# A hybrid encoder layer on one NeuronCore: the order of the attention stage made by a list scheduler inside the kernel

## The chip, the core and the metric

The kernel runs on one core of one Trainium2 chip. The metric is the device time of one execution in microseconds, taken as the median of several runs. One execution was also recorded by the hardware profiler; its span runs from the first recorded instruction to the last and is a little shorter than the time of that execution. Engines are called PE (matmul), ACT, DVE, POOL and SP; SP only issues transfers here, and ACT and POOL issue some too.

## The reference, cut to what matters

One encoder layer in float32 over two requests, 512 and 256 tokens of width 2048, with shared weights. The 768 tokens are handled together as six blocks of 128 rows.

```python
h = rmsnorm(x); z = h @ w_in                      # columns: fourier 1024 | q 1024 | k 256 | v 256
of = einsum('bsgc,gcd->bsgd', fft2(zf).real, w_f) # 8 groups of 128 channels
s  = q @ k.T * 64**-0.5, masked to |i-j| <= 128   # 16 q heads, 4 kv heads, head_dim 64, rotary
m  = max(s, sink); p = exp(s-m) / (sum(exp(s-m)) + exp(sink-m)); oa = p @ v
x  = x + concat(rmsnorm(of), rmsnorm(oa)) @ w_out
h  = rmsnorm(x); x = x + relu(h @ w_up)**2 @ w_down   # d_ff = 8192
y  = rmsnorm(x)
```

## The kernel before, in words

Every float32 operand is split into two parts, high and low, whose sum is the value (`split`, L62: ACT writes the high part, DVE the difference). A product is then three matmuls: high by high, high by low, low by high.

The stages follow each other in time. Up to about 399 us PE makes the projections (L481). Beside them DVE, ACT and POOL do the Fourier groups (`fold`, `stage1`, `stage2`), whose results go to DRAM (`of_d`, L347), and the rotation of keys and queries. From 399 to 634 us runs the attention stage (L501 to L739). From 634 to 780 us comes the second half of the output projection (L780), then the up projection (L888) and the down projection (L1163), both in a form with seven products instead of eight.

In the attention stage PE has two kinds of work. The first half of the output projection, the part that takes the Fourier result, is 24 slots (four column blocks `n` by six row blocks `m`) of 24 matmuls each: eight steps `k` of three (L693). It needs nothing from attention and fills PE between the attention pieces. Attention is 24 units, a unit being one block of 128 queries with one kv head, four q heads. In a unit PE makes the scores (`qk`, L522), DVE adds the mask and takes the row maximum (L535), ACT takes the exponentials (L552), DVE sums and inverts (L562), POOL normalises (L565), PE transposes each key block (`trans`, L577), ACT and DVE split it (L580, L581), and PE multiplies it with the values (`pv`, L596). Blocks at the edges of a request see two key blocks of 128, the others three: 16 units have two, 8 have three, 56 key blocks in all. The low half of the result is added to the high half by ACT and DVE (L603, L606) and stored (`oa_d`). When the four units of a row block are stored, `load_oa` (L626) reads it back, splits it and sums its squares for the norm.

The order before: PE's order is the order of the program text everywhere, SP's also in this stage, and the other engines are ordered by the framework. The text order comes from a heap of events with fixed times counted in steps `k` of the projection (`at`, `later`, `run_events`, L651 to L680): unit `u` starts at step 7.52 `u`, its transposes 8.38 steps later, and so on. After every step of three matmuls, the events due are issued.

PSUM has eight banks. Before, the scores of a head take one of four banks `s`; the transposes `t` and the result `o` share two banks (tag `t`); the projection has two (`mm`).

The Fourier result is read back as float32 (`load_of`, L682, tile `ofr`) and split in the attention stage. The queries of three of the four kv heads lie in DRAM already split; `load_q` reads them into `rx`, and ACT copies them to `qs` (L440).

At the start of the second half each pair of row blocks (a half-step, `mp`) gets its partial result `y1_d` and the residual `x` by two SP loads, which POOL adds (L798); the sum is needed by DVE at the end of the half-step (L816). At the border from up to down the first unit of down lies in buffers of the up stage (`factor_tile`, L1115); the second is loaded, summed and split in buffers that are free only later (`loads(1)`, `sums(1)`, `lows(1)`).

Of the kernel before, what the change touches and what calls it, by code (L numbers as in the profile page):

```python
# [29 lines left out]
FG = 8  # L30
# [10 lines left out]
def hybrid_encoder(ctx: ExitStack, tc: tile.TileContext, a: dict):  # L41
# [3 lines left out]
    def f32(ap):  # L45
        return ap.bitcast(F32)

# [67 lines left out]
    of_d = dpool.tile([FG * P, T], F32, tag="of", name="ofd")  # L115
    oa_d = [dpool.tile([NH * HD, P], F32, tag=f"oa{i}", name=f"oad{i}") for i in range(NM)]
# [31 lines left out]


    kctx = ExitStack()  # L150
    with ExitStack() as ph:
# [175 lines left out]
        def stage2(g):  # L327
# [18 lines left out]
            nc.scalar.activation(of[:], of[:], AF.Copy, scale=gcat[:, g : g + 1])  # L346
            nc.scalar.dma_start(of_d[g * P : (g + 1) * P, :], of[:])  # L347
# [54 lines left out]
        def queries(g, i, s):  # L402
# [4 lines left out]
            lo = kt["kp"].tile([P, HALF], F32, tag="rl", name="rl")  # L407
            split(hi[:], lo[:], x, HD ** -0.5)
            nc.scalar.dma_start(qr_d[g][0][rs, t0], f32(hi[:]))
            nc.scalar.dma_start(qr_d[g][1][rs, t0], lo[:])  # L410
# [4 lines left out]
        def load_q(u):  # L415
# [3 lines left out]
            x = kt["kp"].tile([P, 4, P], F32, tag="rx", name="rx", bufs=2)  # L419
            state[u] = {"x": x}  # L420
            if g < NKV - 1:
                nc.sync.dma_start(x[0:64], rows(qr_d[g][0]))
                nc.sync.dma_start(x[64:128], rows(qr_d[g][1]))
                return
            y = kt["kp"].tile([P, 4, P], F32, tag="ry", name="ry", bufs=2)
            nc.sync.dma_start(x[0:64], rows(zq_d[g]))
            nc.sync.dma_start(y[0:32], rows(zq_d[g])[32:64])
            nc.sync.dma_start(y[32:64], rows(zq_d[g])[0:32])
            state[u]["y"] = y

        def rotate_q(u):
            b, g = units[u]
            if g == NKV - 1:
                rotate(state[u]["x"][:HD], state[u].pop("y")[:HD], slice(b * P, (b + 1) * P))

        def split_q(u):
            x = state[u].pop("x")
            qs = state[u]["qs"] = kt["kp"].tile([P, 4, P], F32R, tag="qs", name="qs", bufs=2)
            if units[u][1] < NKV - 1:
                nc.scalar.activation(qs[:], x[:], AF.Copy)  # L440
                return
            nc.scalar.activation(qs[0:64], x[0:64], AF.Copy, scale=HD ** -0.5)
            nc.vector.scalar_tensor_tensor(
                out=qs[64:128], in0=x[0:64], scalar=HD ** -0.5, in1=f32(qs[0:64]), op0=ALU.mult, op1=ALU.subtract
            )
# [20 lines left out]
        for u in range(2):  # L466
            after(32.5 + u, lambda u=u: (load_q(u), split_q(u)))
# [41 lines left out]
    def key_blocks(b):  # L509
        lo, hi = (0, 3) if b < 4 else (4, 5)  # L510
        return max(lo, b - 1), min(hi, b + 1)

    def qk(u, heads):
        b, g = units[u]
        k0, k1 = key_blocks(b)
        nk = (k1 - k0 + 1) * P
        st = state[u]
        for h in heads:
            s = pp3.tile([P, 512], F32, tag="s", name="s", bufs=4)
            st[f"s{h}"] = s  # L520
            for n, kd in enumerate((kdl, kdh)):
                nc.tensor.matmul(s[:, :nk], st["qs"][:, h, :], kd[:, g, k0 * P : k0 * P + nk], start=(n == 0), stop=(n == 1))  # L522

    def row_max(u, heads):
        b, g = units[u]
        k0, k1 = key_blocks(b)
        nk = (k1 - k0 + 1) * P
        off = (k0 - b + 1) * P
        st = state[u]
        if "mx" not in st:  # L530
            st["mx"] = ap_.tile([P, 4], F32, tag="mx", name="mx")
        mx = st["mx"]
        for h in heads:
            s = st[f"s{h}"]
            nc.vector.tensor_tensor_reduce(  # L535
                out=s[:, :nk], in0=s[:, :nk], in1=mask[:, off : off + nk], scale=1.0,
                scalar=sink[:, 4 * g + h : 4 * g + h + 1], op0=ALU.add, op1=ALU.max, accum_out=mx[:, h : h + 1],
            )

    def exps(u):  # L540
        b, g = units[u]
# [814 lines left out]
```

## Time and profile before

| | us |
|---|---|
| median of 3 runs (lowest, highest) | 2648.18 (2647.71, 2649.71) |
| the profiled execution, its own time | 2648.75 |
| its span | 2647.0 |
| PE busy in the span | 2604.1 (98%) |
| DVE, ACT, POOL busy | 1729.4, 1059.4, 260.2 |
| attention stage on PE | 399.4 to 634.0 |
| granted PE clock, mean | 0.997 |

How to read it: a matmul's recorded duration is longer than its distance to the next, since matmuls overlap, so PE is busy in the record even where it is issued late. The spacing of starts tells more than the busy share. A row of the timeline shows the start, the duration, the engine, the line and the operation; in square brackets stands the idle time before it and what ended that.

### The profile page before, as it was taken

Reading aid. Unit: us, or ns where it says so; the run is one execution under the profiler, and the core shown is the slowest. Engines: PE = TensorE matmul, PEld = TensorE weight load, DVE = VectorE, ACT = ScalarE, POOL = GpSimd, SP = SyncE. Lnnn points to the kernel's source line nnn. Section 1 sums busy time; section 2 is a strip of 40 time slices with the busy share of each in tenths; the row PEclk is TensorE's granted clock in tenths of the full one; section 3 lists DMA queues with packets and bytes.
Section 4 is the critical chain, followed back from the end, with each engine's and each line's share of the span. In section 5 each row is a group of like instructions: output and inputs, shape, how many; then the busy total and the mean of one; then the engine's idle time right before and its main releaser. Section 6 shows DMA issues by size and latency. Waiting matters only on the chain.

```text
span 2647.0 us, 35016 instructions
## 1 busy us (share of the span) xinstructions
PE 2604.1 (98%) x13652; PEld 2375.5 (90%) x13652; DVE 1729.4 (65%) x2100; ACT 1059.4 (40%) x1523; POOL 260.2 (10%) x369
## 2 busy tenths in 40 slices
PE   8999999998999999999999999999999999999998
PEld 8999997877889999999999999978888888888886
DVE  6334456766746655555787778757776775777677
ACT  5233326664423343333445444433333333333335
POOL 1011212334310010100000000020000000000000
PEclk9999999999999999999999999999999999999999
DMA  5323465444564454547666666585553672554364
GB/s 172 122 94 110 134 203 153 121 128 149 198 216 165 165 178 158 191 160 270 227 228 219 216 225 234 179 332 175 175 171 100 207 258 68 179 184 158 101 207 145
DMA packets 263398, 468.31 MB, mean 177 GB/s; under 512 B 26240, under 2 KB 157824, under 8 KB 262464
## 3 DMA queue, kind: packets, MB, share of 16 engines
q1 hardware_dynamic: 199232, 314.26, 37.2%
q10 hardware_dynamic: 51792, 101.73, 10.0%
q0 software_dynamic: 12208, 50.08, 5.6%
q8 instruction: 107, 1.75, 0.3%
q14 instruction: 59, 0.48, 0.1%
HBM read 345.67 MB, written 120.32 MB: 176 GB/s over the span
## 4 chain that ended last, share of the span: by engine, by line
PE 75%; DMA 4%; DVE 3%; issue 3%; ACT 1%; POOL 1%; SPq 1%; ACTq 0%; POOLq 0%; DVEq 0%
PE pd L1163 34%; PE pu L888 34%; PE pm L693 6%; PE o L596 1%; PE t L577 1%; PE s L522 1%; DMA ry<-zq 1%; DMA ofr<-ofd 1%; ACT p L552 1%; DMA zq<-zs 0%; DVE s L535 0%; DMA oar<-oad 0%; PE ptx L131 0%; DMA raw<-in_w_out 0%; DMA qh<-rh 0%
## 5 line engine op out<-in xcount | busy, mean ns | idle before, releaser
L888 PE MATMUL pu<-xf,wh 128*128 128x384 f32 x3328 | 848.7, 336 | 0.0
L888 PEld LDWEIGHTS pu<-xf,wh 128*128 128x128 f32 x3328 | 600.5, 188 | 1.8 <-ACT o L906 1.3
L888 PE MATMUL pu<-xf,wl 128*128 128x384 f32 x1664 | 559.1, 336 | 0.0
L1163 PE MATMUL pd<-wl,sh 128*128 128x512 f32 x1332 | 518.9, 390 | 2.4 <-DVE wl L1152 2.4
L1163 PE MATMUL pd<-wh,sl 128*128 128x512 f32 x1332 | 518.9, 390 | 1.5 <-DVE sl L1153 1.5
L1163 PE MATMUL pd<-wh,sh 128*128 128x512 f32 x1332 | 518.9, 390 | 0.0
L1142 ACT ACTIVATE wh<-rd 128x1024 fp32r<-128x1024 f32 x200 | 201.9, 1054 | 531.0 <-PE pd L1163 436.0
L1152 DVE TENSOR_TENSOR wl<-rd,wh 128x1024 fp32r<-128x1024 f32 x200 | 236.0, 1221 | 234.2 <-ACT wh L1142 233.6
L868 ACT ACTIVATE wh<-ur 128x1024 fp32r<-128x1024 f32 x160 | 169.9, 1062 | 374.2 <-PE pu L888 214.1
L888 PEld LDWEIGHTS pu<-xf,wl 128*128 128x128 f32 x1664 | 312.8, 188 | 0.0
L1163 PEld LDWEIGHTS pd<-wl,sh 128*128 128x128 f32 x1332 | 250.4, 188 | 55.0 <-DVE wl L1152 2.8
L1163 PEld LDWEIGHTS pd<-wh,sl 128*128 128x128 f32 x1332 | 250.4, 188 | 53.9 <-DVE sl L1153 1.8
L1163 PEld LDWEIGHTS pd<-wh,sh 128*128 128x128 f32 x1332 | 250.3, 188 | 51.9
L874 DVE TENSOR_TENSOR wl<-ur,wh 128x1024 fp32r<-128x1024 f32 x160 | 195.5, 1222 | 82.6 <-ACT wh L868 82.5
L909 DVE TENSOR_TENSOR o<-pu,o 128x768 f32<-128x768 f32 x160 | 153.0, 956 | 116.9 <-PE pu L888 111.1
L481 PE MATMUL pz<-hh,wh 128*128 128x384 f32 x576 | 147.1, 336 | 0.0
L481 PE MATMUL pz<-hl,wh 128*128 128x384 f32 x576 | 146.3, 334 | 0.0
L481 PE MATMUL pz<-hh,wl 128*128 128x384 f32 x576 | 146.2, 334 | 0.0
L1135 DVE TENSOR_TENSOR rd<-rd 128x1024 f32<-128x1024 f32 x112 | 131.8, 1218 | 0.0
L868 ACT ACTIVATE wh<-sx 128x1024 fp32r<-128x1024 f32 x64 | 67.9, 1062 | 127.8 <-PE pu L888 97.0
L66 DVE TENSOR_TENSOR wl<-raw,wh 128x1024 fp32r<-128x1024 f32 x56 | 68.8, 1235 | 65.8 <-ACT wh L65 63.2
L1153 DVE TENSOR_TENSOR sl<-sr,sh 128x768 fp32r<-128x768 f32 x111 | 105.6, 951 | 0.0
(208 smaller groups left out, 3558.8 us busy)
## 6 DMA issues: line engine op xcount, KB each, us to landing
rd<-in_w_down SPq DMA_DIRECT2D x176, 512.0 KB, 5.1
ur<-in_w_up SPq DMA_DIRECT2D x128, 512.0 KB, 3.9
sr<-sd SPq DMA_DIRECT2D x95, 384.0 KB, 5.3
pd<-o ACTq DMA_DIRECT2D x64, 384.0 KB, 2.3
o<-pd POOLq DMA_DIRECT2D x64, 384.0 KB, 6.1
sd<-sm ACTq DMA_DIRECT2D x60, 384.0 KB, 2.9
raw<-in_w_in SPq DMA_DIRECT2D x40, 512.0 KB, 3.6
raw<-in_w_out SPq DMA_DIRECT2D x32, 512.0 KB, 5.0
```

What stands on the lines that cost most here:

```text
L66: nc.vector.tensor_tensor(out=lo, in0=src, in1=f32(hi), op=ALU.subtract)
L481: nc.tensor.matmul(ps[c][s][:, :HALF], w[:, i, cs], h[j][:, i, s * HALF : (s + 1) * HALF], start=first and n == 0, stop=last and n == 2,)
L693: nc.tensor.matmul(ps[:], l(k), w[:, k % 2, :], start=(k == 0 and n == 0), stop=(k == 7 and n == 2))
L868: nc.scalar.activation(wh[:], raw[:], AF.Copy)
L874: nc.vector.tensor_tensor(out=wl[:], in0=raw[:], in1=f32(wh[:]), op=ALU.subtract)
L888: nc.tensor.matmul(ps[:, t, :HALF], w[:, i, t * P : (t + 1) * P], xb[:, o, i, :], start=(s == first_of[bank] and i == 0 and n == 0), stop= ...
L909: nc.vector.tensor_tensor(out=o, in0=src, in1=o, op=ALU.add)
L1135: add = lambda x, y, op: nc.vector.tensor_tensor(out=x[:], in0=x[:], in1=y[:], op=op)
L1142: nc.scalar.activation(wh[:], t[:], AF.Copy)
L1152: nc.vector.tensor_tensor(out=wl[:], in0=t[:], in1=f32(wh[:]), op=ALU.subtract)
L1153: nc.vector.tensor_tensor(out=sl[:], in0=sr[:], in1=f32(sh[:]), op=ALU.subtract)
L1163: nc.tensor.matmul(ps[m][:, ns], l[:, q, ts], w[:, ns], start=(j == 0 and q == 0 and t == 0), stop=(j == HP // 2 - 1 and q == 1 and t == 2),)
```

## The change

It has five parts.

1. The attention stage gets a list of jobs. A job has a key, an engine, a cost in us, a due time, a function, the jobs it comes after, an earliest start and a wait until its result can be used. `in_turn` makes a list schedule of them while the program is built (at each step the job that can start first, ties by due time), and the jobs are issued in that order. In this stage ACT, DVE, POOL and SP now follow the text order too, not PE and SP alone. The pieces of a unit become single jobs, four row maxima, four exponentials and so on. The negated maxima are made in two instructions of two columns, not one of four.
2. PSUM: the scores have three banks, and a unit with two key blocks puts two heads into one bank; `o` has a bank of its own, the transposes two.
3. The Fourier result is split in `stage2` and stored as two tensors, which the attention stage loads straight into place. Queries that lie split in DRAM are loaded straight into `qs` (three buffers). The attention result is stored in two unadded halves; `oa_load` loads one and adds the other on the way by an accumulating transfer of the POOL queue. The partial results `y1` are stored by SP.
4. In the second half the residual is loaded by SP, and `y1` is added on it by an accumulating transfer of the POOL queue.
5. Down's second unit is loaded into buffers of up, summed and half split before down begins; two weight pieces that are kept for later are loaded a second time.

The diff, cut ("..." marks what is left out):

```diff
-    of_d = dpool.tile([FG * P, T], F32, tag="of", name="ofd")
-    oa_d = [dpool.tile([NH * HD, P], F32, tag=f"oa{i}", name=f"oad{i}") for i in range(NM)]
+    of_d = [dpool.tile([P, NM, FG, P], F32, tag=f"of{c}", name=f"ofd{c}") for c in "hl"]
+    oa_d = [[dpool.tile([NH * HD, P], F32, tag=f"oa{c}{i}", name=f"oad{c}{i}") for c in "hl"] for i in range(NM)]
...
-            nc.scalar.activation(of[:], of[:], AF.Copy, scale=gcat[:, g : g + 1])
-            nc.scalar.dma_start(of_d[g * P : (g + 1) * P, :], of[:])
+            split(ofh[:], ofl[:], of[:], gcat[:, g : g + 1])
+            for c, x in enumerate((ofh, ofl)):
+                nc.scalar.dma_start(of_d[c][:, :, g, :], f32(x[:]).rearrange("p (m t) -> p m t", m=NM))
...
         for u in range(2):
-            after(32.5 + u, lambda u=u: (load_q(u), split_q(u)))
+            after(32.5 + u, lambda u=u: load_q(u))
+        for i in range(2):
+            after(32.5 + i, lambda i=i: (out_load(i), out_split(i)))
...
+    def maxima(u, step):
...
+            hs = slice(2 * step, 2 * step + 2)
+            nc.vector.tensor_scalar(out=st["nm"][:, hs], in0=st["mx"][:, hs], scalar1=-1.0, scalar2=None, op0=ALU.mult)
...
+    def oa_load(m, c):
+        for i in range(2):
+            src = oa_d[m][c][i * 512 : (i + 1) * 512, :].rearrange("(k p) t -> p k t", p=P)
+            if c == 0:
+                oar[m, i] = (op, ap_)[i].tile([P, 4, P], F32, tag="oar", name="oar", bufs=2)
+                nc.sync.dma_start(oar[m, i][:], src)
+            else:
+                nc.gpsimd.dma_start(oar[m, i][:], src, accum_op=ALU.add)
...
+    def load_of(m):
+        for c in range(2):
+            nc.sync.dma_start(f32(ofs[m][c][:]), of_d[c][:, m])
...
+    def in_turn(hop, slack):
...
+        while ready:
+            key = min(ready, key=lambda x: (max(ready[x], free.get(jobs[x][0], -1e9)), jobs[x][2], number[x]))
+            engine, cost, _, _, _, _, wait = jobs[key]
+            t = starts[key] = max(ready.pop(key), free.get(engine, -1e9))
+            free[engine], ends[key] = t + cost, t + cost + wait
+            order.append((t, len(order), key))
+            for x in users[key]:
+                blocked[x] -= 1
+                if not blocked[x]:
+                    late = hop + (slack if jobs[x][0] == PE and x[0] != "mm" else 0)
+                    ready[x] = max([jobs[x][5]] + [starts[a] if o else ends[a] + late for a, o in needs[x]])
+        return [key for _, _, key in sorted(order)]
+
+    PACE, SLOT = 8.8, 9.75
...
+                job(
+                    ("mm", n, m, k), PE, 0.69, 1e6, lambda n=n, m=m, k=k: slot_step(n, m, k),
+                    *((("mm", n, m, k - 1),) if k else (("xc", *before(2)), ("mm", *before(1), 7), ("of", m))),
+                    ("lo", 4 * n + k // 2), start=0, wait=0.2,
+                )
...
+        for h in range(4):
+            job(("n", u, h), POOL, 0.6 if wide else 0.48, t0 + 5, lambda u=u, h=h: normalize(u, h), ("rs", u))
...
+        job(("a0", m), SP, 1.6, due, lambda m=m: oa_load(m, 0), *(("put", 4 * m + g) for g in range(4)), ("or", m - 2), wait=4)
+        job(("a1", m), POOL, 2.4, due, lambda m=m: oa_load(m, 1), ("a0", m), wait=6)
+        for i in range(2):
+            job(("ph", m, i), ACT, 0.62, due + 5, lambda m=m, i=i: oa_part(m, i, 0), ("a1", m), ("mm", 3, m - 1, 7), ("ph", m, i - 1))
+            job(("pl", m, i), DVE, 0.65, due + 6, lambda m=m, i=i: oa_part(m, i, 1), ("ph", m, i))
...
+    with tc.manual_schedule(engines=by_hand):
+        for key in in_turn(0.05, 0.4):
+            jobs[key][3]()
...
-        load_oa(5)
...
-                    nc.sync.dma_start(yp[:, s, :], y1_d[m][n][:])
-                    xr = op.tile([P, 4, P], F32, tag="oar", name="xr", bufs=2)
-                    xr_ = xr[:].rearrange("p k t -> p (k t)")
-                    nc.sync.dma_start(xr_, x_rows(m)[:, n * 512 : (n + 1) * 512])
-                    nc.gpsimd.tensor_tensor(out=yp[:, s, :], in0=yp[:, s, :], in1=xr_, op=ALU.add)
+                    nc.sync.dma_start(yp[:, s, :], x_rows(m)[:, n * 512 : (n + 1) * 512])
+                    nc.gpsimd.dma_start(yp[:, s, :], y1_d[m][n][:], accum_op=ALU.add)
...
+        if i == 4 and k in (2, 3):
+            return down_piece(k, 1, 1, early=True), None
...
-        if u == 0:
+        if u < 2:
             return up.tile([P, 2, HALF], dt, tag="o", name="o" + what, bufs=10)
...
             if u == UL and s == 5:
                 sums(0)
                 lows(0)
+                loads(1)
             if u == UL and s == 6:
                 up_after(UL, 0)
+                sums(1)
+                lows(1, (0,))
...
     products(0, ps, 0)
     up_out(UL, 6)
+    lows(1, (1,))
...
-    loads(1)
     loads(2)
-    sums(1)
+    for k in (2, 3):
+        kept[k] = down_piece(k, 1, 1)
...
-        if u + 1 < len(dunits):
+        if 0 < u and u + 1 < len(dunits):
             lows(u + 1)
```

479 lines of the change are left out of this document (281 added, 198 removed).

## The prediction

> **What bounds the kernel now.** I read the stretches first, to see in which stage PE is not fed. The columns are the stretch, its length, busy time (instructions) of PE, weight loads, DVE, ACT and POOL, the granted PE clock, the DMA share and GB/s.
>
> ```profile
> core 0 of [0], span 2647.0 us
> 0.00:399.40 399.40, 390.86 (x2456) 388.56 (x2457) 184.97 (x323) 130.27 (x235) 51.09 (x54) 1.00 0.44 140
> 399.40:419.00 19.60, 15.86 (x67) 11.48 (x66) 13.19 (x33) 10.88 (x24) 3.12 (x5) 0.91 0.85 267
> 419.00:617.00 198.00, 190.24 (x985) 156.00 (x984) 142.71 (x380) 131.27 (x337) 67.37 (x105) 1.00 0.39 114
> 617.00:634.00 17.00, 13.69 (x58) 10.91 (x57) 10.04 (x16) 8.94 (x19) 5.47 (x8) 0.90 0.40 121
> 399.40:634.00 234.60, 219.79 (x1106) 178.39 (x1105) 165.95 (x428) 151.08 (x376) 75.96 (x117) 0.99 0.43 127
> 634.00:681.00 47.00, 43.42 (x207) 35.38 (x206) 26.03 (x41) 16.63 (x29) 18.00 (x17) 1.00 0.63 209
> ```
>
> The attention stage lasts 234.6 us and no engine but PE is over 71% busy in it (DVE 165.95). PE is idle 14.8 us there, and in its first and last stretch the clock was granted at 0.91 and 0.90.
>
> Busy time hides more, since matmuls overlap. So I take the distance from start to start of each kind of matmul where PE streams. The chain of waits gives three kinds (start, length, what), the timeline the two sizes of scores.
>
> ```profile
> 439.50 0.93 PE o L596 x4
> ...
> 740.00 10.90 PE pm L693 x48
> 750.90 0.87 PE ptx L131 x8
> ```
>
> ```profile
> 403.61 0.28 PE L522 MATMUL s<-kdl,qs 128*128 128x256 f32 x1
> ...
> 404.07 0.40 PE L693 MATMUL pm<-wh,ofh 128*128 128x512 f32 x1
> ...
> 446.75 0.34 PE L522 MATMUL s<-kdl,qs 128*128 128x384 f32 x1
> ...
> 447.44 0.39 PE L693 MATMUL pm<-wh,ofh 128*128 128x512 f32 x1
> ```
>
> Projection 10.90/48 = 0.227 us, values 0.93/4 = 0.2325, transposes 0.87/8 = 0.109 (those of the second half have the same 128x128 shape), scores of 256 columns (404.07 - 403.61)/4 = 0.115, of 384 columns (447.44 - 446.75)/4 = 0.172. The code gives the counts: 24 slots x 24 = 576 projections, 56 key blocks x 2 = 112 value matmuls and x 4 = 224 transposes, 128 scores of 256 columns and 64 of 384. The sum is 130.8 + 26.0 + 24.4 + 14.7 + 11.0 = **206.9 us**. The stage takes 234.6, so **27.7 us** are lost. From the stretches, idle plus slow clock: the start lost 3.7 + 0.09 x 15.9 = 5.2, the end 3.3 + 0.10 x 13.7 = 4.7; the middle has the other 17.8, of which 7.8 are recorded as idle and the rest are late starts that hide under a neighbour's duration.
>
> Next, what PE waited for in the stage; the group of the transposes (busy, mean ns | idle before, releasers) names it.
>
> ```profile
> L577 PE MATMUL t<-ident,p 128*128 128x128 f32 x224 | 35.7, 279 | 9.7 <-DVE os L606 8.0 <-POOL p L565 1.1
> ```
>
> The largest wait has one cause: transposes need a PSUM bank that `o` holds until DVE's sum `os` has read it (8.0 of the 14.8 us idle).
>
> **Part 1 and 2: order and banks.** `o` gets a bank and `os` goes, so the 8.0 us of that wait cannot recur in this form; DVE loses the 24 sums:
>
> ```profile
> L606 DVE TENSOR_TENSOR os<-o,ob 64x512 f32<-64x512 f32 x24 | 16.3, 679 | 1.6 <-ACT ob L603 1.5
> ```
>
> PE's matmuls are the same in number and size, so the floor stays 206.9. Can the other engines follow at the new pace? DVE had 166 us of work and keeps some 150 without the sums, in some 219 us that is 68%; ACT had 151 and loses the copies of the queries. So PE remains the bound, and what is left is timing. The plan's costs agree with the rows (projection step 0.69 against 3 x 0.227 = 0.68; four transposes 0.44 against 4 x 0.109), and it gives each attention job on PE 0.4 us of slack. What it cannot know is single late hand-offs, and on a PE that follows its text in order each of them is paid. I estimate 0.3 us per unit, 24 x 0.3 = 7 us for the middle. Bounds: 3 (a third of the recorded idle time stays) and 17.8 (the new order is no better). The gain is 10.8.
>
> The start: before, the timeline shows
>
> ```profile
> 400.55 0.39 PE L522 MATMUL s<-kdl,qs 128*128 128x256 f32 x1 [0.71 <-DVE zs L493]
> ...
> 402.01 0.50 PE L693 MATMUL pm<-wh,ofh 128*128 128x512 f32 x1 [0.96 <-ACT ofh L65]
> ...
> 413.04 1.78 PE L577 MATMUL t<-ident,p 128*128 128x128 f32 x4 [1.06 <-POOL p L565]
> ```
>
> The first wait (a PSUM bank of the projection) stays. The second goes if the split Fourier result is in place by then: its loads may start once the memory under `ofs` is free, which held the first quarter of the projection's input and is read last by the fourth piece from the end. The third was followed by the slow clock; with two weight pieces split earlier the projection can fill that place. I take 1.5 us instead of 5.2; bounds 0.7 and 5.2. The end: the last unit still runs through seven hand-offs with few projection steps left to cover them; 4.0 instead of 4.7, bounds 2 and 4.7. The stage then loses 7 + 1.5 + 4 = 12.5: 219.4 us, **a gain of 15.2**.
>
> **Part 3: Fourier and attention output in two parts.** DVE gets eight more 128x768 differences, 8 x about 0.95 us, in the first stretch above, where it is busy 185 of 399 us; PE's projections cover them, and without that cover they would cost 7.6 us. The second store per group adds an issue on ACT's queue there (ACT is 130 of 399 busy). Nothing is charged. On the other side the attention stage loads the parts with twice the bytes, 6 x 1 MB at a DMA share of 0.43.
>
> The accumulating transfers are new, and no row shows one. The nearest rows are plain loads of the POOL queue; the page says for a load of 384 KB (us to landing), and the group of down's residual loads, with DMA saturated:
>
> ```profile
> o<-pd POOLq DMA_DIRECT2D x64, 384.0 KB, 6.1
> ```
>
> ```profile
> L1243 POOL DMA_DIRECT2D acc<-x x24: 537/537/544, 1725.4 to 1752.9; - x24
> ...
> DMA to landing us min/median/max: 5.6/10.4/12.2
> ```
>
> The plan reckons 6 us. I take 6.1 and keep 12.2 as the far end (5.6 the near one); the stretch has a DMA share of 0.43, far from saturation. Behind it waits ACT's `ph`, and behind that all of ACT's exponentials, so lateness here is a rival below. POOL itself waits for `oa_load`'s first half, with the normalisations queued behind it. Issue takes POOL 0.54 us each.
>
> A rule speaks against putting these on POOL. The Trainium skill (SBUF — State Buffer, "The 'DVE blocks DMA' trap") says that POOL writes the descriptors of such transfers and is locked out while DVE runs in a two-port mode. Its figure, 620 ns growing to about 3100 ns, would as an estimate make each accumulation 2.5 us later. The issue times above do not show it (537 to 544 ns), so the sum has nothing for it.
>
> **Part 4: residual.** Before, PE stood for the first sum of the second half:
>
> ```profile
> 653.88 1.22 PE L131 MATMUL ptx<-ident,yp 128*128 128x128 f32 x8 [2.32 <-DVE yp L816]
> ```
>
> ```profile
> 645.50 1.28 POOL L640 TENSOR_TENSOR oar<-oar 128x512 f32<-128x512 f32 x1
> 649.93 2.51 POOL L798 TENSOR_TENSOR yp<-yp,xr 128x512 f32<-128x512 f32 x2 [3.16 <-DMA xr<-in_x_prompt]
> ```
>
> `xr` shared its buffers with the last row block's `oar`, so POOL added only at 649.9. Now `x` can be loaded as soon as the last slot frees `yp`: about 3 us (the wait above) and 6.1 for the accumulation, 643 instead of 652.4. The stretch from 634 to 681 is idle 47.0 - 43.4 = 3.6 us; I leave 0.8, **a gain of 2.8** (bounds 3.6, and a loss of 6.6 by the second rival). Later half-steps hide the transfers under some 23 us of projection.
>
> **Part 5: down's second unit.**
>
> ```profile
> 1723.59 0.96 DVE L923 TENSOR_TENSOR sm<-o 128x768 f32<-128x768 f32 x1 [3.66 <-DMA sd<-sm]
> 1724.46 2.35 DVE L1152 TENSOR_TENSOR wl<-re,wh 128x1024 fp32r<-128x1024 f32 x2
> ```
>
> ```profile
> 1722.96 0.39 PE L1163 MATMUL pd<-wh,sh 128*128 128x512 f32 x1
> ...
> 1732.17 0.39 PE L1163 MATMUL pd<-wh,sl 128*128 128x512 f32 x1
> ```
>
> DVE's difference `sm` waited for a store to free its buffer, and unit 1's `wl` stood behind it in DVE's order. Between the two PE rows lie 14 matmuls, worth 14 x 0.227 = 3.2 us; they took 9.2. In the new text unit 1's differences come before that `sm`, within the 8.2 us of unit 0's 36 matmuls. That loss is 6.0 us; **gain 5.5**, keeping 0.5 because unit 2 is late next: its `wl` stands behind the same `sm` now, and PE wants it 8.2 us after 1723. Bounds 3 and 6. The two repeated weight loads have no place on the path.
>
> **The sum.** 15.2 + 2.8 + 5.5 = 23.5. The profiled execution took 2648.75 (span 2647.0 and 1.75 around it), 0.57 over the median 2648.18. 2648.18 - 23.5 = 2624.7, so **2624.7 us**.
>
> **The rivals.**
>
> First, accumulations land late. Row blocks 0, 3 and 4 are read back without a slot to wait for, so ACT meets the landing itself. At 12.2 us instead of 6 that holds ACT three times by 6.2, 18.6 us: 2643. For it: the 12.2 above. Against: DMA was saturated there. Chance 0.12.
>
> Second, POOL issues the first residual accumulations behind the last row block's squares. Those ended at 646.8 and now come 6.1 later for their own accumulation, then another 6.1: 659.0 instead of 652.4, 6.6 us more stall instead of 2.8 less: 2634. For it: POOL's order before was squares, then residual. Against: the squares are ready later than the residual load. Chance 0.12.
>
> Third, slower: POOL's normalisation and DVE's small maxima block each other.
>
> ```profile
> L549 DVE TENSOR_SCALAR nm<-mx x24: 149/158/1157, 406.5 to 615.3; 128x4 f32<-128x4 f32 x24
> ```
>
> ```profile
> L565 POOL TENSOR_SCALAR p<-p,rs x96: 471/480/1592, 412.5 to 620.2; 128x256 f32<-128x256 f32 x64, 128x384 f32<-128x384 f32 x32
> ```
>
> Both have maxima far above their medians (ns), and the change makes two `nm` per unit instead of one, each ahead of the exponentials. If a tight order puts every unit into the worst case, it costs (1157 - 158) + (1592 - 480) ns less the slack of 0.4, 1.7 us x 24 = 41 us instead of my 7: 2659. It decides from (7 + 23.5)/24 = 1.3 us per unit, where all that is forecast is given back. Against: the medians say that few were hit. The Trainium skill (SBUF — State Buffer, "Who interferes with whom") has DVE's `tensor_scalar` among the instructions that take the port pair shared with POOL; the two maxima agree. Chance 0.10.
>
> Fourth, the scheduler's order is no better than the heap's: start, middle and end lose what they lost (15.2 of the gain gone), and the second rival takes its 9.4 us. Then 23.5 - 15.2 - 9.4 = -1.1, 2649, no difference. For it: the old order too was laid out with times for each step, and lost 27.7. Against: its largest wait came from the bank, which is gone. Chance 0.06.
>
> **How the numbers follow.** My forecast has 0.60. Its own range is 2613 (3 + 0.7 + 2 left of the stage's loss, so 22.0 gained there, 3.6 and 6.0 elsewhere: 31.6; and 3 more if the middle loses nothing) to 2635 (17.8 stays in the middle, the rest as forecast: 2635.5). Reaching to the first two rivals, the range is 2613 to 2644; outside are the third and fourth and little else. A measurement of this kernel tells about 0.2%, 5 us, from no change. Faster is the forecast and the first two rivals, 0.84; the same 0.06; slower 0.10.
>
> **What would show it.** Right: the stage from first score to first matmul on `oa` takes 216 to 223 us; waits of `t` on `os` are gone; granted clock near 1.00 in the first 20 us; no gap before the first transposes `ptx`; 14 matmuls after unit 0 of down in about 3.2 us. Wrong: ACT's `ph` waiting several us for an accumulation, POOL's squares ahead of the residual, `nm` or `p` with means near their former maxima, or unit 2 of down stalling for what unit 1 gained.

## The result, and the profile after

The changed kernel takes 2633.16 us (median of 4 runs, 2631.49 to 2635.16), the kernel before beside it 2648.59 us (2647.71 to 2649.71): a ratio of 0.9943, 95% interval 0.993 to 0.9955, or 15.4 us less. The forecast was 2624.7, 23.5 us less; the range of 2613 to 2644 holds the result. The profiled execution took 2635.16 us (span 2633.4, so 13.6 below the span before).

The stretches of the changed kernel, with the columns of the same view before: length, busy time (instructions) of PE, weight loads, DVE, ACT and POOL, granted clock, DMA share, GB/s. The cuts are those of before, moved to the first score matmul (401.6) and the first projection on `oah` (625.2).

```profile
401.60:419.00 17.40, 15.22 (x68) 11.99 (x67) 10.05 (x31) 7.57 (x21) 2.57 (x5) 0.90 0.88 286
419.00:607.00 188.00, 184.94 (x964) 153.81 (x963) 127.92 (x377) 119.61 (x320) 75.30 (x114) 1.00 0.57 153
607.00:625.20 18.20, 17.41 (x79) 13.65 (x78) 7.71 (x11) 7.82 (x13) 10.23 (x12) 1.00 0.83 175
401.60:625.20 223.60, 217.57 (x1107) 179.45 (x1106) 145.68 (x419) 135.00 (x353) 88.10 (x126) 0.99 0.61 165
625.20:672.00 46.80, 43.21 (x201) 34.39 (x199) 24.39 (x41) 15.17 (x26) 19.17 (x22) 1.00 0.79 193
```

The stage takes 223.6 us, 11.1 less than before. Of its loss over the floor (223.6 - 206.9 = 16.7), idle time plus slow clock puts 2.2 + 0.10 x 15.2 = 3.7 at the start and 0.8 at the end; the middle keeps 12.2. And the stage begins 2.1 us later.

That way of counting gives the middle everything that hides under a neighbour's duration in the other two stretches. The other way takes the distance from the start of each matmul to the next start, less the floor of its kind. By it the start, the middle and the end lose 5.3, 9.6 and 1.7 us after, and 7.7, 14.9 and 5.2 before. Put down to the kind of matmul that came next, the losses of the whole stage are (us; worked out from the start times in the traces):

| what PE came to | before | after | x1 | x2 | x8 |
|---|---|---|---|---|---|
| first transpose behind other work | 11.3 | 2.4 | 1.0 | 2.7 | 2.8 |
| transpose behind a transpose | 2.1 | 5.7 | 2.2 | 5.6 | 13.5 |
| projection | 8.1 | 5.2 | 13.7 | 7.4 | 5.9 |
| scores | 2.5 | 2.2 | 8.4 | 3.2 | 1.9 |
| value sum | 3.7 | 1.1 | 9.0 | 7.7 | 0.3 |

x1, x2 and x8 are runs of the next section.

The stages of all profiles, by first and last matmul: first score; from there to the first projection on `oah` (stage); from there to the first of up (second half); from the first of down to the last. The second column is the median time, the third the ratio to the kernel before with its interval.

| kernel | us | ratio | first score | stage | second half | down |
|---|---|---|---|---|---|---|
| before | 2648.59 | | 399.5 | 234.7 | 146.4 | 919.7 |
| after | 2633.16 | 0.9943 (0.993 to 0.9955) | 401.6 | 223.6 | 148.6 | 913.7 |
| x5, after again | 2633.85 | 0.9943 (0.9931 to 0.9956) | 401.5 | 222.7 | 147.5 | 913.7 |
| x1, banks alone | 2657.84 | 1.003 (1.0019 to 1.0042) | 400.1 | 241.3 | 149.0 | 921.1 |
| x2, list on PE alone | 2650.04 | 1.0004 (0.9995 to 1.0013) | 401.2 | 233.6 | 153.7 | 913.6 |
| x3, residual by sums | 2635.84 | 0.9947 (0.9934 to 0.9961) | 400.4 | 223.2 | 148.3 | 913.7 |
| x4, down undone | 2638.62 | 0.9959 (0.9946 to 0.9971) | 402.0 | 222.6 | 144.5 | 919.9 |
| x6, rows of 2 KB | 2634.84 | 0.9945 (0.9932 to 0.9957) | 402.6 | 222.2 | 146.0 | 913.6 |
| x7, weights later | 2634.38 | 0.9943 (0.993 to 0.9955) | 400.3 | 224.3 | 148.4 | 913.7 |
| x8, hop -0.1 | 2651.33 | 1.0012 (1.0002 to 1.0021) | 402.5 | 231.4 | 155.8 | 913.7 |
| x9, last landing 11 | 2633.33 | 0.9936 (0.9923 to 0.995) | 400.3 | 225.8 | 145.8 | 913.7 |
| x10, slack 0.8 | 2636.87 | 0.9948 (0.9936 to 0.9961) | 400.8 | 223.4 | 151.3 | 913.7 |
| x11, three edits | 2631.25 | 0.9929 (0.9916 to 0.9941) | 400.5 | 222.9 | 144.6 | 913.7 |
| x12, x11 and hop 0.15 | 2638.75 | 0.9961 (0.9948 to 0.9975) | 401.2 | 225.3 | 149.2 | 913.7 |

From before to after this gives 2.1 - 11.1 + 2.2 - 6.0 = -12.8; up gives 0.4 and the tail 0.3. It also tells how far one profile can be trusted: the second half is the same code in after, x4, x5 and x7 and takes 144.5 to 148.6 us; down takes 913.6 or 913.7 us in every profile with the new code and 919.7 to 921.1 with the old.

The transposes' group (busy, mean ns | idle before, releasers), which led the list of waits before with 9.7 us, 8.0 of it on `os`:

```profile
L632 PE MATMUL t<-ident,p 128*128 128x128 f32 x224 | 33.8, 280 | 3.2 <-POOL p L624 1.7
L733 PE MATMUL pm<-wl,ofh 128*128 128x512 f32 x192 | 75.6, 394 | 1.5 <-DVE wl L183 1.5
```

The wait on `os` is gone; POOL's probabilities and DVE's weight splits are next. The start of the stage, PE's timeline:

```profile
406.95 0.40 PE L733 MATMUL pm<-wh,ofh 128*128 128x512 f32 x1
408.07 0.50 PE L733 MATMUL pm<-wl,ofh 128*128 128x512 f32 x1 [0.73 <-DVE wl L183]
...
411.70 2.53 PE L632 MATMUL t<-ident,p 128*128 128x128 f32 x8 [1.07 <-POOL p L624]
...
415.31 0.63 PE L733 MATMUL pm<-wl,ofh 128*128 128x512 f32 x1
415.74 0.63 PE L733 MATMUL pm<-wh,ofl 128*128 128x512 f32 x1
```

The first projections no longer wait for `ofh`, but the first unit's transposes still wait for POOL, and behind that wait the matmuls follow at 415.74 - 415.31 = 0.43 us instead of 0.23. The second half's first sums, by the chain of waits (start, length, what):

```profile
623.93 10.05 DMA oar<-oadl
...
634.00 0.63 ACT oah L690
634.63 0.62 ACT wh L167
...
635.27 2.21 DVE wl L178 x2
...
637.50 0.38 SPq L77
...
637.92 5.63 DMA yp<-in_x_sample
643.56 0.29 issue
643.85 0.85 POOL yp L938
644.70 0.60 POOL r L99
...
645.33 0.76 DVE yp L956
```

The first of the last row block's two accumulating transfers lands 10.05 us after its issue. ACT waits for it with a weight split queued behind, DVE's split follows, SP's weight load waits for that split, the next half-step's load of `x` stands behind the weight load, POOL's accumulation waits for `x`, and behind it on POOL stands the power that makes `r2`, which the first half-step's sum needs.

### The profile page after: what moved, and what is told of

It is laid out like the page before. It is cut to its first block, busy times and chain, and to the rows that moved or that the text cites. A ratio compares the mean times of both kernels' runs of the same rounds, so it can differ in the third digit from the quotient of the medians.

```text
span 2633.4 us, 35140 instructions
## 1 busy us (share of the span) xinstructions
PE 2600.9 (99%) x13652; PEld 2374.8 (90%) x13652; DVE 1711.7 (65%) x2102; ACT 1042.5 (40%) x1499; POOL 269.7 (10%) x381
## 4 chain that ended last, share of the span: by engine, by line
PE 73%; DMA 1%; DVE 1%; issue 1%; POOL 0%; ACT 0%; POOLq 0%; SPq 0%; ACTq 0%; DVEq 0%
PE pu L1028 35%; PE pd L1309 34%; PE pm L733 4%; DMA oar<-oadl 0%; PE ptx L133 0%; DMA yp<-in_x_prompt 0%; DMA yp<-in_x_sample 0%; DVE acc L1243 0%; DMA x<-yp 0%; DVE acc L1230 0%; DVE wl L178 0%; POOL yp L938 0%; DVE acc L1408 0%; POOL r L99 0%; DVE yp L956 0%
## 5 line engine op out<-in xcount | busy, mean ns | idle before, releaser
L1309 PE MATMUL pd<-wh,sh 128*128 128x512 f32 x1320 | 513.5, 389 | 0.0
L1309 PE MATMUL pd<-wl,sh 128*128 128x512 f32 x1320 | 513.5, 389 | 0.0
L1309 PE MATMUL pd<-wh,sl 128*128 128x512 f32 x1320 | 513.5, 389 | 0.0
L536 PEld LDWEIGHTS pz<-hh,wl 128*128 128x128 f32 x576 | 103.9, 188 | 0.6 <-DVE wl L68 0.6
```

The source lines that it names most:

```text
L536: nc.tensor.matmul(ps[c][s][:, :HALF], w[:, i, cs], h[j][:, i, s * HALF : (s + 1) * HALF], start=first and n == 0, stop=last and n == 2,)
L1309: nc.tensor.matmul(ps[m][:, ns], l[:, q, ts], w[:, ns], start=(j == 0 and q == 0 and t == 0), stop=(j == HP // 2 - 1 and q == 1 and t == 2),)
```

## The experiments

**Banks alone, and the order on PE alone.** x1 is the kernel before with the new banks (the negated maxima and exponentials must then go in two halves); x2 is the kernel after with the list's order on PE and SP only.

```diff
-            s = pp3.tile([P, 512], F32, tag="s", name="s", bufs=4)
+            if nk > 256 or h % 2 == 0:
+                s = pp3.tile([P, 512], F32, tag="s", name="s", bufs=3)
...
-            st["o"] = pp3.tile([P, 512], F32, tag="t", name="o", bufs=2)
+            st["o"] = pp3.tile([P, 512], F32, tag="o", name="o", bufs=1)
```

> The kernel before with only the banks changed: the value sums get a bank of their own, the scores three banks (two heads of 256 columns share one), and with that the negated maxima and exponentials go in two halves; the sum os and the old order of events stay. If the bank did most of the attention stage's gain of 11.1 us, the 8.0 us of waits of the transposes for os go and the stage takes 225 to 228 us: about 2640 us in all. If the new order did it, the waits move on to another hand-off (probabilities late on POOL, or score matmuls waiting for their bank) and the stage stays at 232 us or more: 2646 us or more.

```diff
-    with tc.manual_schedule(engines=by_hand):
+    with tc.manual_schedule(engines={mybir.EngineType.SP}):
         for key in in_turn(0.05, 0.4):
```

> The kernel after, but the list scheduler's order is kept on PE and SP alone; ACT, DVE and POOL are ordered by the framework as before the change. If the order on these three engines matters (ACT's and DVE's splits of weights and the maxima must come when the list has them), the stage of 223.6 us grows by 5 us or more: 2638 us or more. If PE's order and the banks are all of it, the time stays within 2 us of the changed kernel's 2633.

x1 is slower than before: its stage takes 241.3 us, 6.6 more. PE's groups in the stage show the waits that came instead:

```profile
L699 PE MATMUL pm<-wh,ofh 128*128 128x512 f32 x192 | 81.9, 427 | 4.3 <-ACT ofh L65 3.8 <-ACT wh L65 0.6
L583 PE MATMUL t<-ident,p 128*128 128x128 f32 x224 | 35.8, 281 | 0.4
L524 PE MATMUL s<-kdl,qs 128*128 128x256 f32 (+1 forms) x96 | 28.6, 312 | 4.9 <-ACT p L557 4.9
L602 PE MATMUL o<-tl,vhl 128*128 128x512 f32 x56 | 23.3, 417 | 3.4 <-DVE tl L587 3.4
L602 PE MATMUL o<-th,vhl 128*128 128x512 f32 x56 | 22.7, 405 | 2.4 <-ACT th L586 2.4
```

The transposes wait 0.4 us instead of 9.7, as the bank promised, but the scores wait 4.9 for the exponentials that must empty their third bank, the value sums 5.8 for the splits, and the projections 4.3 for the split of the Fourier result. In x2 the stage takes 233.6 us, 10.0 more than in the first profile of after; the same value sums wait again:

```profile
L632 PE MATMUL t<-ident,p 128*128 128x128 f32 x224 | 33.3, 280 | 4.6 <-POOL p L624 3.5 <-DVE tl L641 0.4
L649 PE MATMUL o<-tl,vhl 128*128 128x512 f32 x56 | 22.8, 407 | 4.1 <-DVE tl L641 4.0
```

So neither the banks with the old order nor the list on PE and SP alone brings the gain of 11 us. It needs the list's order on ACT, DVE and POOL too: in x2 DVE has a reduction (`sr`, 1.05 us at 469.3), a weight split (`wl`, 1.22 at 534.6) or a product of the rotation (`rx`, 0.68 at 552.2) just ahead of a late difference `tl`. Of x2's time 5 us more lie in the second half (153.7). No run has the full list with the old banks, or part 3 undone, so the share of these two in the gain is not shown.

**Residual and down.** x3 puts back the two loads and POOL's sum of part 4, x4 undoes part 5.

```diff
-                    nc.sync.dma_start(yp[:, s, :], x_rows(m)[:, n * 512 : (n + 1) * 512])
-                    nc.gpsimd.dma_start(yp[:, s, :], y1_d[m][n][:], accum_op=ALU.add)
+                    nc.sync.dma_start(yp[:, s, :], y1_d[m][n][:])
+                    xr = op.tile([P, 4, P], F32, tag="oar", name="xr", bufs=2)
...
+                    nc.gpsimd.tensor_tensor(out=yp[:, s, :], in0=yp[:, s, :], in1=xr_, op=ALU.add)
```

> The kernel after with part 4 undone: two SP loads and a POOL sum make the residual again. By the prediction's step (the accumulating transfer saves 2.8 us) the time grows to about 2636. If instead the accumulating transfers are what makes the first sums late (PE's gaps of 1.5 us at 644.5 and 1.6 us at 671.6), the second half's 148.7 us come down to about 146.6: 2631. If the late read-back of the last row block is the cause, the second half stays within 1 us of 148.7: 2633.

The time is 0.9947 of before, against 0.9943: no difference that can be measured, and the second half's 148.3 us lie among those with the accumulation. The 2635.8 us are near the expected 2636, but not by the step that was tested: in this profile 2.2 us more than in the changed kernel lie behind down's last matmul (see the last section). No gain or loss by part 4 is shown.

```diff
-        if u < 2:
+        if u == 0:
             return up.tile([P, 2, HALF], dt, tag="o", name="o" + what, bufs=10)
...
-                loads(1)
...
-                sums(1)
-                lows(1, (0,))
...
-    lows(1, (1,))
...
+    loads(1)
     loads(2)
-    for k in (2, 3):
-        kept[k] = down_piece(k, 1, 1)
+    sums(1)
```

> The kernel after with part 5 undone: down's second unit is loaded, summed and split behind the border again. By the prediction's step the 6.0 us between unit 0's last and unit 1's next matmuls come back: 2639 us, and the border shows 14 matmuls in 9.2 us. If the gain between down's first matmul and the last (903.1 to 897.1) has another source, the time stays within 2 us of 2633.

Down takes 919.9 us instead of 913.7, and the whole 2638.6. PE at its border in x4:

```profile
1711.21 0.39 PE L1307 MATMUL pd<-wh,sh 128*128 128x512 f32 x1
1714.09 0.50 PE L1307 MATMUL pd<-wl,sh 128*128 128x512 f32 x1 [2.49 <-DVE wl L1294]
1716.10 0.64 PE L1307 MATMUL pd<-wh,sl 128*128 128x512 f32 x1 [1.50 <-DVE sl L1297]
1716.54 0.63 PE L1307 MATMUL pd<-wh,sh 128*128 128x512 f32 x1
...
1719.52 0.48 PE L1307 MATMUL pd<-wl,sh 128*128 128x512 f32 x1
```

and in the changed kernel, unit 1's first, its fifteenth and unit 2's first matmul:

```profile
1715.74 0.39 PE L1309 MATMUL pd<-wh,osh 128*128 128x512 f32 x1
...
1718.91 0.39 PE L1309 MATMUL pd<-wh,osl 128*128 128x512 f32 x1
...
1723.90 0.39 PE L1309 MATMUL pd<-wh,sh 128*128 128x512 f32 x1
```

Fourteen matmuls take 3.17 us, and unit 2 follows without a wait: 36 matmuls in 8.16 us.

**The changed kernel again, and three edits that each touch one suspect.**

> The changed kernel once more, unedited, as the measure for the runs beside it and for how far two profiles of the same code differ. If the second half's 148.6 us (before: 146.4) are the work of the change, this profile shows them within 1 us again. If they are chance (the profile without part 5, whose second half is the same code, shows 144.5), it lands anywhere from 144 to 149. Time 2633, stage 222.5 to 224.

The second half takes 147.5 us, within the spread and with the same chain of waits (the first of the last two accumulations lands 9.39 us after its issue there).

```diff
-                oa_d[b][c][g * 256 : (g + 1) * 256, :].rearrange("(h d) t -> d h t", d=HD), ob[c * HD : (c + 1) * HD]
+                oa_d[b][c][r * HD : (r + 1) * HD, 2 * g : 2 * g + 2], ob[c * HD : (c + 1) * HD, r : 4 : 2]
...
-            src = oa_d[m][c][i * 512 : (i + 1) * 512, :].rearrange("(k p) t -> p k t", p=P)
+            src = oa_d[m][c][:, 4 * i : 4 * i + 4]
```

> The kernel after with another layout of the attention output in DRAM: the read-back takes one piece of 2 KB for each partition instead of four of 512 bytes (the stores write the same pieces of 512 bytes, in four transfers a unit instead of two). If the small pieces make the accumulating transfers slow (issue on POOL 1.27 to 1.86 us, landing 4.7 to 12.1 us), the issue falls to about the 0.88 us of the residual's rows of 2 KB and the landing to 4 to 5 us, and the waits of oah (5.7 us) go: 2629 to 2632. If PE does not wait behind them, issue and landing fall and the time stays within 2 us of the changed kernel.

The accumulating transfers of the read-back, issue (ns, min/median/max) and landing, in the changed kernel and then in x6:

```profile
L682 POOL DMA_DIRECT2D oar<-oadl x12: 1269/1546/1855, 449.8 to 624.9; - x12
...
DMA to landing us min/median/max: 4.7/6.6/12.1
```

```profile
L683 POOL DMA_DIRECT2D oar<-oadl x12: 882/1124/1237, 451.2 to 624.1; - x12
...
DMA to landing us min/median/max: 4.4/6.0/8.5
```

The small pieces do cost issue time and a late landing at the end, but the time (0.9945) does not move; 1.8 us of it lie behind down's last matmul, as in x3.

```diff
-            after(32.5 + i, lambda i=i: (out_load(i), out_split(i)))
+            after(35, lambda i=i: (out_load(i), out_split(i)))
```

> The kernel after, but the first two pieces of the output weights are loaded and split behind the last projection piece, as before the change, not at 32.5 and 33.5. If they delay the last projection pieces (gaps of some 1 us at 391 to 393), the first score comes at about 400.4 instead of 401.6 us, but the projection's first steps then wait for their weights at 403 to 405, as in the kernel before (start loses 5.2 instead of 3.7): total 2632 to 2635. If the early pieces cost nothing, the first score stays at 401.6 and the time is 2635.

The first score comes at 400.3 us and the stage takes 224.3; the sum, 624.6, is that of after (625.2) and x5 (624.2). In the changed kernel PE stands twice near the end of the projection, and in x7 it doesn't:

```profile
392.64 0.62 PE L536 MATMUL pz<-hh,wh 128*128 128x384 f32 x2 [0.40 <-ACT wh L67]
...
393.90 0.62 PE L536 MATMUL pz<-hh,wl 128*128 128x384 f32 x2 [0.30 <-DVE wl L68]
```

ACT makes the projection's last weight split at 391.54 us there, behind one of the early pieces (379.32); in x7 it makes it at 368.07. The last 81 matmuls ahead of the first score take 14.04 us in x7, before and x1, 15.3 in after and x5, and 14.4 to 16.2 in the other profiles with the early pieces. So the early pieces cost about 1.2 us here, and the stage gains about as much. That x3, x9 and x11 have 400.3 to 400.5 in spite of them has two reasons: they cost only 0.4 to 0.9 us there, and the start of the kernel varies. Its 126th matmul starts anywhere from 26.5 to 28.5 us in the profiles with the new projection code, and at 27.0 and 27.7 in the two with the old.

**The list's own numbers.**

```diff
-        for key in in_turn(0.05, 0.4):
+        for key in in_turn(-0.1, 0.4):
```

> The kernel after with one number of the list scheduler changed: the time it adds at each hand-off goes from 0.05 to -0.1 us, which takes away its own wait of 0.1. The list then places a job as soon as the rows' durations allow it. If the 16.7 us that the stage still loses come from an order laid out for hand-offs slower than the chip's, the stage falls to 220 us or less and the whole to 2629 or less. If they come from single late hand-offs that no order foresees, a tighter list makes PE wait more often: the stage grows to 226 us or more, 2636 or more.

All the gain is lost: 2651.3. Against the profile of the changed kernel, 7.8 us more lie in the stage, 7.2 in the second half and 0.8 ahead of the first score. In the stage the transposes wait 9.0 us again, now 6.8 of it for POOL's `p`; their group, and then one unit of x8, POOL and DVE:

```profile
L632 PE MATMUL t<-ident,p 128*128 128x128 f32 x224 | 36.1, 281 | 9.0 <-POOL p L624 6.8 <-DVE tl L641 0.4
```

```profile
602.69 3.29 POOL L624 TENSOR_SCALAR p<-p,rs 128x256 f32<-128x256 f32 x4 [2.26 <-ACT qs L493]
```

```profile
602.62 0.69 DVE L496 SCALAR_TENSOR_TENSOR qs<-rx,qs 64x512 fp32r<-64x512 f32 x1
603.72 1.53 DVE L692 TENSOR_TENSOR oal<-oar,oah 128x512 fp32r<-128x512 f32 x2 [0.41 <-ACT oah L690]
```

Four normalisations of 0.48 us should take 1.9 and take 3.29, beside DVE instructions that read two operands in SBUF. The Trainium skill (SBUF — State Buffer, "Who interferes with whom") has such a DVE instruction contend with a POOL instruction that reads SBUF; these rows agree. So do the other normalisations: in all fourteen profiles the 718 of 256 columns that run beside none of DVE's large instructions of this kind (`rx`, `qs`, `wl`, `oal`, `ofl`), nor behind a transfer issue of POOL's own, take 0.47 to 0.51 us. In x8, 13 of 64 take 0.72 to 3.04 us, each of them beside such an instruction; in the changed kernel three take 0.77 to 0.92. No run takes these instructions away, so the link rests on this coincidence.

In the second half of x8 stands the order of the prediction's second rival. The last row block's accumulations are issued only at 640.37 us, its squares follow, and the residual's accumulations come behind the last square:

```profile
654.14 1.26 POOL L701 TENSOR_TENSOR oar<-oar 128x512 f32<-128x512 f32 x1
655.34 2.65 POOL L938 DMA_DIRECT2D yp<-y  x3
```

```profile
660.49 1.09 PE L133 MATMUL ptx<-ident,yp 128*128 128x128 f32 x4 [9.65 <-DVE yp L956]
```

```diff
-        for key in in_turn(0.05, 0.4):
+        for key in in_turn(0.05, 0.8):
```

> The kernel after with the scheduler's slack for attention jobs on PE at 0.8 us instead of 0.4. If late hand-offs to PE (3.2 to 3.7 us of waits of the transposes, 1.5 us for weights) are what is left and the list lays them out too close, the stage falls below 222 us and the time to 2631 or less. If the list's outcome is as good as chance around this point (-0.15 us a hop cost 8.7 us in the stage), the stage may land anywhere from 222 to 232 and the waits of the transposes for p don't shrink.

The stage does not move (223.4 us); the transposes wait 2.5 us and the scores 1.8 for ACT's exponentials. In the second half PE is idle 5.3 us ahead of the first `ptx`: 2636.9. There the last row block's transfers land after 4.5 and 7.6 us, and the load of `x` is late: 10.37 us instead of the 5.63 above.

```diff
-        job(("a1", m), POOL, 2.4, due, lambda m=m: oa_load(m, 1), ("a0", m), wait=6)
+        job(("a1", m), POOL, 2.4, due, lambda m=m: oa_load(m, 1), ("a0", m), wait=11 if m == NM - 1 else 6)
```

> The kernel after, with one number of the list changed: for the last row block alone the scheduler reckons 11 us instead of 6 from the accumulating transfer's issue to its landing (9.4 and 11.1 us in the two profiles of this code). ACT's order then has the weight split that stood behind the last row block's oah ahead of it. If that chain (transfer, ACT oah, ACT wh, DVE wl, SP weight load, SP x load, POOL accumulation, POOL r, DVE yp, PE ptx) is what holds the second half, the gaps of 0.5 to 1.6 us at 634 and of 1.2 to 2.8 us ahead of ptx shrink and the second half takes 145 us or less instead of 147.5 and 148.6: about 2631. If the transfers' own landing sets the end whatever stands behind it, the second half stays within 1 us.

The second half takes 145.8 us, between the two expectations, but the time's ratio (0.9936, interval 0.9923 to 0.995) is not told apart from 0.9943. x11 adds the rows of 2 KB and POOL's order of the text:

```diff
-    with tc.tile_pool(name="pp4", bufs=1, space=PSUM, reuse_waits="tile") as pp:
+    with tc.tile_pool(name="pp4", bufs=1, space=PSUM, reuse_waits="tile") as pp, tc.manual_schedule(
+        engines={mybir.EngineType.Pool}
+    ):
```

> Three edits together: the 2 KB rows of the read-back, the last row block's landing reckoned at 11 us, and POOL's order in the second half as the text has it, so that r2's power is no longer queued behind the next half-step's accumulations. By the chain that the profiles show, the second half loses its gaps ahead of the first ptx: 144.5 us or less and 2630 in all. If the last transfer's landing alone sets it, 146 us (as with the rows alone) and 2634.

2631.25 us (2630.09 to 2632.04), with 144.6 in the second half; its first stretch, to be held against the 43.21 of 46.80 us after:

```profile
623.40:670.20 46.80, 44.99 (x214) 36.72 (x214) 29.14 (x46) 17.96 (x32) 17.83 (x21) 1.00 0.81 209
```

PE is idle 1.8 us there instead of 3.6. The best time measured, 1.9 to 2.6 us below the changed kernel's; the ratios' intervals overlap, and x4 has 144.5 without any of these edits, so a gain by them is not shown.

> The kernel of the three edits together (2 KB rows, last landing at 11 us, POOL's order of the text; stage 222.9 us there), with the scheduler's hand-off at 0.15 us instead of 0.05: the other way from the run with -0.1, where the transposes waited 9.0 us and the stage took 231.4. If longer hand-offs in the plan leave PE more covered, the waits of the transposes fall below 3.1 us and the stage below 222: 2630 or less. If 0.05 is near the best, or the outcome of a list is as good as chance, the stage comes to 224 to 232 us and the time to 2633 or more.

The edit is `in_turn(0.15, 0.4)` in x11. The stage grows to 225.3 us, the second half to 149.2, the time to 2638.75; the transposes wait 7.8 us, 6.5 for `p`. With one list tried of each, a longer and a shorter hand-off are both worse than 0.05.

## Why the prediction was right, and where it was wrong

**The sign, and the term of the stage.** The floor of 206.9 us and the lost 27.7 were the right place: the stage gave 11.1 and 12.0 us in the two profiles, where 15.2 stood. Of its three losses the start was priced at 1.5 and was 3.7, the middle at 7 and was 12.2, the end at 4.0 and was 0.8 (from start to start: 5.3, 9.6 and 1.7). That the stage misses by no more than 4.2 is in part luck: the end made up for some of the other two. The start's mistake is a step: "with two weight pieces split earlier the projection can fill that place". The projection ran to 406.95, waited for the low half of the fourth weight piece, and then the first unit's transposes waited for `p`; the slow clock followed as before. The middle's 0.3 us a unit was an estimate without a row. One part of what is there is POOL's issue of the accumulating transfers. Put at 0.54 us each, it takes 1.27 to 1.86 (0.88 to 1.24 with the rows of 2 KB in x6), and normalisations queue behind it:

```profile
531.17 2.63 POOL L682 DMA_DIRECT2D oar<-oadl  x2 [6.48 <-issue]
532.79 2.85 POOL L624 TENSOR_SCALAR p<-p,rs 128x256 f32<-128x256 f32 x4
```

```profile
534.38 2.09 PE L632 MATMUL t<-ident,p 128*128 128x128 f32 x8 [0.23 <-POOL p L624]
536.22 0.48 PE L733 MATMUL pm<-wh,ofh 128*128 128x512 f32 x1
```

The eight transposes take 1.84 us to the next start; at the floor's 0.109 each they need 0.87. Shorter issues in x6 did not change the stage beyond its spread (222.2), so this is a small part. The largest part is the same hand-off without that issue: half of what the whole stage still loses stands at the transposes (8.1 of 16.5 us, table above). 5.7 of it lie between two transposes, most of it where PE is early and takes the heads' `p` one by one, as POOL finishes them some 0.45 us apart. Another 5.2 lie ahead of projections, where the rows name late weight splits. So "single late hand-offs" was the right kind of loss, and it was priced too low.

Of the signs that were named, the waits on `os` are gone and the stage is at the edge of 216 to 223 us; the clock of the first stretch (0.90, not near 1.00), the gap ahead of the first `ptx` and ACT's wait for the last accumulation spoke against their steps, as said there.

**What made the stage faster.** The prediction gave it to banks and order together and reasoned mostly from the bank: "the 8.0 us of that wait cannot recur in this form". That held, and was worth less than nothing by itself (x1): the wait went on to the next releasers, scores, value sums and projections.

**Part 3, charged at nothing.** The first score came 2.1 and 2.0 us later. Over the eleven profiles with the changed projection code as it stands it comes at 401.3 in the mean (400.3 to 402.6), against 399.5 and 400.1 with the old: 1.5 us. The split and the second store, which the prediction left uncharged, cost next to nothing: from the 126th to the 2376th matmul it takes 358.57 us in after and x5 and 358.43 before. What cost is the early weight pieces, 1.2 us at the end of the projection (x7), and the prediction had these as a gain alone. The rest of the 2.1, some 0.8 us, falls ahead of the 126th matmul, where x1 with the old code is late by 0.7 too.

**Part 4, +2.8.** Nothing came of it: with the same list the second half takes 144.5 to 148.6 us with accumulation and 148.3 without (146.4 and 149.0 with the old order). The wrong step is "6.1 for the accumulation, 643 instead of 652.4". What holds the first sums in the changed kernel is the last row block's transfer, issued in a stretch with a DMA share of 0.83 (607.00 to 625.20), and it holds `x` through weight splits and SP's queue. In after, x5 and x7 it lands after 10.0, 9.4 and 8.7 us, with 148.6, 147.5 and 148.4 in the second half; in x4 after 6.6 us, with 144.5. In x10 the load of `x` itself was late. Of a general lateness of the accumulations, by the 2.5 us that the prediction names as a rule's estimate, the median landing of 6.6 us shows little: 6.1 was reckoned. The first rival had that mechanism and looked for it in row blocks 0, 3 and 4; the far bound of 12.2 was the nearer row (10.0 and 12.1 us for the last pair). The second rival's order (squares ahead of the accumulations) did not occur in the changed kernel, though it did in x8: POOL issued the first accumulation ahead of the squares, and what stood wrongly on POOL was an accumulation ahead of `r2`'s power.

**Part 5, +5.5.** Right: 6.0 us, and x4 gives them back. Unit 2, for which 0.5 us were kept, was not late.

**The third rival** read two maxima as one effect, and the traces before don't show that. The 1592 ns of `p` ran beside DVE's differences `wl` and `oal`, and the 1157 ns of `nm` beside POOL's squares. After the change `nm` was never above 0.57 us. The normalisations of 256 columns went from

```profile
L565 POOL TENSOR_SCALAR p<-p,rs 128x256 f32<-128x256 f32 x64 | 31.8, 515 | 81.3 <-ACT th L580 39.6 <-DVE rs L563 27.1 <-PE s L522 8.7
```

to

```profile
L624 POOL TENSOR_SCALAR p<-p,rs 128x256 f32<-128x256 f32 x64 | 32.6, 628 | 70.5 <-DVE rs L620 28.9 <-ACT xc L746 20.7 <-PE s L578 7.5
```

The mean rose from 515 to 628 ns, but by eight records behind a transfer issue that overlap each other; the busy time, which counts overlaps once, rose by 0.8 us in the whole stage. What PE still waits for is when the normalisations come; that they take longer shows in x8, beside DVE's sums and differences.

**The fourth** (the list is no better than the heap) is refuted as the change stands, but x8 ends where that rival does, one number away: 2651.

## What to carry to other kernels

The list scheduler paid here only when it ordered every engine that hands work to the bound one: with PE and SP alone the stage gave back ten of eleven us. Its outcome hangs on the numbers for hand-offs, and here these were found by runs. Idle time in the record understates the waits of overlapping matmuls; from start to start 8.1 us were lost at the transposes after the change, where the record has 3.2 as idle. When a wait is named for one releaser, ask what the next releaser is before its whole length is booked as gain; and price a transfer by its slowest row where it stands last in a stage, not by its median. One profile of a stage that hangs on transfers may be off by 4 us; a change of 2 us there takes repeated profiles.

## What the runs showed of the hardware

A stall can cost more than its idle time. In x4 PE is idle 2.5 and 1.5 us at down's border, and then 512-column matmuls start 0.427 us apart for 3.4 us (1716.10 to 1719.52) before they are back at 0.227; of the 6.0 us some 1.6 are this slow clock. The Trainium skill (TensorE: Matmul & The Clock Gate, Part 1) says that the array runs at half its clock after idling until some 3.4 us of work have passed; these rows agree. It puts a whole idle window of some 3.4 us ahead of the slow clock; the start of the stage after agrees less. There 1.07 us of waiting and then transposes 0.46 us apart, which leaves PE standing for some 2.3 us between 410.4 and 413.1, were followed by spacings of 0.43. The 1 us lost at 534.38 had no such sequel.

An accumulating transfer cost POOL more issue time here than a plain one of the same shape: for rows of 2 KB the residual's `yp<-y` take 0.88 us (0.85 at the least) and the plain `acc<-x`, in another stage, 0.537 (0.546 at the most), and with pieces of 512 bytes it is 1.27 us at the least. What part of that is DVE's doing is not shown.

The profiles of x3, x6, x11 and x12 run on some 2 us longer behind down's last matmul than the others of this change (13.9 to 14.3 us to the end, against 12.1). The time goes into POOL's last wait behind the same store: its DRAIN takes 7.15 us in x6 and 5.34 in after. Why is open.
